# First layer's MLP in two phases of block products, by way of DRAM, and pooling evicted straight to its result

## The chip, the core and the metric

The kernel runs on one core of one Trainium2 chip. The metric is the device time of one execution in microseconds (us), median over runs. TensorE (PE in the profile) multiplies matrices into PSUM; VectorE (DVE), ScalarE (ACT) and GpSimd (POOL) do the elementwise work; SyncE (SP) only issues DMAs.

## The reference

Two layers act on 512 latent and 256 context tokens of width 1024, in fp32. The parts that the change touches:

```python
def multiscale_pool(u, w_grp, scale):            # windows 2, 4, 8, 16; one per group of 128 channels
    ug = u.reshape(B, L, POOL_GROUPS, POOL_GW)
    ...                                          # cs: running sums along the tokens
        means.append((csg[:, hi] - csg[:, lo]) / (hi - lo).astype(F32)[:, None])
    pooled = jnp.stack(means, axis=2).astype(u.dtype)
    mixed = jnp.einsum('blgc,gcd->blgd', pooled - ug, w_grp)

def sq_relu_mlp(h, w1, w2):                      # w1: 1024 x 4096, w2: 4096 x 1024
    return jnp.square(jax.nn.relu(h @ w1)) @ w2

for l in range(DEPTH):                           # DEPTH = 2
    ...                                          # mixers: retention, pooling, attention, then w_out
    x = x + g1 * mix
    x = x + g2 * sq_relu_mlp(modulate(rmsnorm(x, norm2_w[l]), sh2, sc2), w_mlp1[l], w_mlp2[l])
    if not last:                                 # the same for the context tokens
        xc = xc + cg2 * sq_relu_mlp(modulate(rmsnorm(xc, norm2_w[l]), csh2, csc2), w_mlp1[l], w_mlp2[l])
```

## The kernel before

Every fp32 product is three matmuls (`mm3`, L309): each operand is split into a rounded high part (`wh`, `uh`, made by ACT) and the rest (`wl`, `ul`, made by DVE or POOL), and high x high, high x low and low x high are added in PSUM.

`Weights` (L95) streams all weights in the order of a plan. `next` hands out the slab of the step that begins, issues the DMAs up to three steps ahead on SP's queue, and lines up the splits up to two steps ahead; `tick`, called between products, emits one piece of such a split: an ACT copy (L150) and a subtraction (L151), each 512 wide. `combine` (L163) forms sums of weight blocks on POOL, 1024 wide. Raw slabs have 6 buffers, `wh` and `wl` 3 each. Large tiles come from a pool of 11 buffers (`big`).

In layer 0 all 768 tokens go through the MLP. The hidden width 4096 is cut into 8 chunks of 512. `mlp_order` (L212) alternates: `m1` makes one chunk of the first product (per weight slab of 128 hidden channels, 8 contraction tiles, for 512 and for 256 tokens; tile `ph`, ACT evicts, squares), then `s2` (`strassen`, L1205) multiplies the chunk by its part of `w_mlp2` as 2x2 blocks in 7 block products in place of 8 (tile `st`, operands `ob`, added into `acc` by DVE). Chunks 6 and 7 go through `m2` without that. `fold` adds the result to the residual. The context and latent rows are parked in DRAM (`xk`) and read back (`xq`).

Ahead of it, output product and norm run in two groups of tiles, (0,1,2,3) and (4,5). `early` lets the MLP's first products, which need group 1 alone, run before group 2 is normalised. Beside the MLP the next layer's modulation weights (`adaw`, 24 loads of 1 MB) are loaded on POOL's queue and multiplied (`ada`).

`pool_gen` (L678) makes the pooling input: per group 48 matmuls into PSUM (`pu`), ACT evicts them to a scratch tile `up` of one buffer (L694), DVE builds window sums from it (`ps`, L703 and L706), scales and subtracts into `pm` (L711) and mends the ends (L714, L715). The next group's eviction needs `up` free.

Of the kernel before, what the change touches and what calls it, by code (L numbers as in the profile page):

```python
# [17 lines left out]
P = 128  # L18
# [14 lines left out]
NSC = 6  # L33

# [14 lines left out]
def kernel(  # L49
# [45 lines left out]
    class Weights:  # L95
# [10 lines left out]
        def add(self, key, src, pre=None, name=None):  # L106
            self.plan.append((key, src if isinstance(src, tuple) else (src,), pre, name or len(self.plan)))
# [15 lines left out]
        def dma(self, upto):  # L123
            while self.nd <= min(upto, len(self.plan) - 1):
                key, src, pre, name = self.plan[self.nd]
                if pre is None:
                    self.load(name, src)
                else:
                    for nm, ap in pre[0]:
                        self.load(nm, (ap,))  # L130
                self.nd += 1

        def split(self, upto):
            while self.ns <= min(upto, len(self.plan) - 1):
                i = self.ns
                src = self.plan[i][1][0]
                m = src.shape[1] * src.shape[2]
                box = {}
                key, _, pre, name = self.plan[i]
                if pre is not None and pre[1]:  # L140
                    self.bg.append((i, lambda pre=pre: self.combine(pre[1])))
                eng = V if key[0] == "s2" or key[0] in ("m1", "m2") and not (key[0] == "m1" and key[1:3] == (1, 0) and key[3] > 1) or key[:2] == ("t", 0) and key[2] < C_AK else nc.gpsimd

                def piece(i=i, a=0, b=512, box=box, eng=eng, name=name):
# [4 lines left out]
                    r = self.raw[name]  # L149
                    A.activation(out=box["h"][:, a:b], in_=r[:, a:b], func=AF.Copy)  # L150
                    eng.tensor_tensor(out=box["l"][:, a:b], in0=r[:, a:b], in1=box["h"][:, a:b].bitcast(F32), op=ALU.subtract)  # L151

                for a in range(0, m, 512):
                    half = key[0] == "out" or key[0] in ("m1", "m2") and key[1] == 0 or key[:3] == ("t", 0, C_RV + 256)
                    e = {"eng": nc.gpsimd if a else V} if half else {}
                    self.bg.append((i, lambda a=a, piece=piece, e=e: piece(a=a, b=a + 512, **e)))
                self.ns += 1

        def combine(self, op):
            o, a, b, f = op  # L160
            t = wp.tile([P, 1024], F32, name=f"wr{self.nr}", tag="raw", bufs=6)
            self.nr += 1
            nc.gpsimd.tensor_tensor(out=t, in0=self.raw[a], in1=self.raw[b], op=f)  # L163
            self.raw[o] = t
# [46 lines left out]

    def mlp_order(l):  # L212
        if l in STR:
            o = [("m1", 0)]
            for ch in range(1, NSC):
                o += [("m1", ch), ("s2", ch - 1)]
            o += [("s2", NSC - 1), ("fold",), ("m1", 6), ("m1", 7)]
            return o + [("m2", 6, g) for g in (NG[0] if l == 0 else mlp2_groups(l, 6))]
        o = []
        for ch in range(8):  # L220
            o.append(("m1", ch))
            if 0 < ch < 7:
                o.append(("m2", ch - 1, mlp2_groups(l, ch - 1)[0]))
        if l == 0:
            o += [("m2", 6, g) for g in NG[0]]
        else:
            o.append(("m2", 6, mlp2_groups(l, 6)[0]))
        return o

    for l in range(DEPTH):  # L230
# [17 lines left out]
        for gr in NG[l]:  # L248
            for cb in range(2):
                for kq in range(4):  # L250
                    W.add(("out", l, gr, cb, kq), wslab(w_out[l], kq * 256, 2, cb * 512, 512))
        for o in mlp_order(l):
            if o[0] == "fold":
                continue
            if o[0] == "s2":
                q = [[wslab(w_mlp2[l], o[1] * CHUNK + kh * 256, 2, c * 512, 512) for c in range(2)] for kh in range(2)]
                nm = lambda x: (l, o[1], x)
                sub, b11, b12, b21, b22, t1, t2, t3, t4 = ALU.subtract, *(nm(x) for x in ("11", "12", "21", "22", "t1", "t2", "t3", "t4"))
                for pq, loads, op, of in ((1, [(b11, q[0][0])], None, b11), (5, [(b12, q[0][1])], (t1, b12, b11, sub), t1),
                                          (6, [(b22, q[1][1])], (t2, b22, t1, sub), t2), (3, [], None, b22),  # L260
                                          (7, [], (t3, b22, b12, sub), t3), (2, [(b21, q[1][0])], None, b21),
                                          (4, [], (t4, b21, t2, sub), t4)):
                    W.add(("s2", l, o[1], pq), q[0][0], (loads, op), of)
# [76 lines left out]
    def ada(l, v, c0, n, ps_pool, ps_tag, wk, loads=None, eng1=None):  # L340
# [4 lines left out]
        if eng1 is not None:  # L345
            g = ada_dve(l, v, c0, wk, eng1)
            while acc is None:
                try:
# [3 lines left out]
                    acc = e.value  # L352
        pa = None
# [6 lines left out]
        for s, (rv, ins) in enumerate(() if acc else loads or ada_load(l, v, c0, n, nc.gpsimd)):  # L360
# [157 lines left out]
    def layer(l, u_in):  # L518
# [159 lines left out]
        def pool_gen(*gs):  # L678
            for g in gs:
                wh, wl = W.next(("pu", l, g))  # L680
                up = wk.tile([P, 800], F32, name=f"up{g}", tag="up", bufs=1)
                V.memset(up[:, 0:8], 0.0)
                V.memset(up[:, 520:536], 0.0)
                if not last:
                    V.memset(up[:, 792:800], 0.0)
                for t0, n in groups:
# [6 lines left out]
                    o = 8 if t0 == 0 else 536  # L693
# [3 lines left out]
                src, lo, hi = up, 0, (536 if last else 800)  # L697
                for s in range(g + 1):
                    st = 1 if s == 0 else 1 << (s - 1)
                    dst = wk.tile([P, 800], F32, name=f"ps{g}{s}", tag=f"pls{s % 2}")  # L700
                    if s == 0:
                        lo += 1
                        V.tensor_tensor(out=dst[:, lo:hi], in0=src[:, lo - 1 : hi - 1], in1=src[:, lo:hi], op=ALU.add)  # L703
                    else:
                        lo, hi = lo + st, hi - st
                        V.tensor_tensor(out=dst[:, lo:hi], in0=src[:, lo - st : hi - st], in1=src[:, lo + st : hi + st], op=ALU.add)  # L706
                    src = dst
                for t0, n in groups:
# [486 lines left out]
        u2h = [bigt(f"u2h{l}{q}", F32R) for q in range(2)]  # L1195
        u2l = [bigt(f"u2l{l}{q}", F32R) for q in range(2)]
# [6 lines left out]
        acc = {}  # L1203

# [149 lines left out]
        for q, gr in enumerate(NG[l]):  # L1354
# [6 lines left out]
        early()  # L1361
# [34 lines left out]
    def norm_mod(ts, xns, q, a, sh, uh, ul, wk, psp, tag):  # L1396
# [3 lines left out]
        u = wk.tile([P, 2, 256], F32, name=f"un{ts[0]}{q}", tag="un", bufs=unb[0])  # L1400
# [15 lines left out]

    def norm_group(ts, xts, a, sh, uh, ul, wk, psp, tag):
# [84 lines left out]
```

## Time and profile before

| | |
|---|---|
| median of 3 runs | 2147.99 us (2147.91 to 2148.69) |
| the profiled execution | 2149.35 us, its span 2147.6 us |
| busy share | PE 97%, weight loads 83%, DVE 61%, ACT 40%, POOL 29% |
| granted TensorE clock, mean | 0.991 |
| layer 0, MLP in full flow (791 to 1235 us) | 444 us |

The trace is of one execution; its rows give start, duration, engine, source line and tile (`out<-in`). A matmul's shown duration covers its way through the array, so neighbouring matmuls overlap in the rows: the pace of PE is the distance from start to start.

### The profile page before, as it was taken

To read this page: it belongs to the slowest core of one execution; us is meant where nothing else is said; L and a number is where in the kernel's file an instruction comes from. 1 tells how busy PE (TensorE), PEld (TensorE's weight loads), DVE (VectorE), ACT (ScalarE), POOL (GpSimd) and SP (SyncE) were. 2 spreads that over 40 slices of the span, in tenths; PEclk is the share of its full clock that TensorE was granted. 3 is DMA by queue.
4 is the path that set the end of the run, shared out by engine and by line. 5 is a ranking of instruction groups with operands and counts; after the bars stand their busy time and mean duration, and the time that the engine had idled before them with its cause. 6 is when DMAs were issued, how large, how long until landed. Compare 5 with 4: busy or idle time off the path is not lost.

```text
span 2147.6 us, 32806 instructions
## 1 busy us (share of the span) xinstructions
PE 2083.2 (97%) x12879; PEld 1775.8 (83%) x12879; DVE 1315.7 (61%) x2542; ACT 856.2 (40%) x1710; POOL 613.4 (29%) x475
## 2 busy tenths in 40 slices
PE   6999979999999999999999999998999999999999
PEld 5789968888888888888888888997888888887777
DVE  4577973455443654446569547479465267778884
ACT  4323423443432354434343335233444345654441
POOL 0342242212223331232322123433323353221300
PEclk9999989999999999999999999999999999999999
DMA  8841111111124444244426233212222164233241
GB/s 267 313 149 49 38 45 50 45 40 50 40 60 160 157 136 148 86 141 128 131 97 214 71 137 108 79 47 60 77 60 70 54 217 122 89 97 118 77 129 49
DMA packets 224692, 225.77 MB, mean 105 GB/s; under 512 B 8417, under 2 KB 180761, under 8 KB 224537
## 3 DMA queue, kind: packets, MB, share of 16 engines
q1 hardware_dynamic: 208936, 168.96, 25.2%
q0 software_dynamic: 15600, 54.71, 7.2%
q8 instruction: 101, 1.65, 0.3%
q14 instruction: 55, 0.44, 0.1%
HBM read 216.27 MB, written 7.37 MB: 104 GB/s over the span
## 4 chain that ended last, share of the span: by engine, by line
PE 80%; DVE 13%; issue 2%; DMA 2%; ACT 2%; SPq 1%; POOL 0%; DVEq 0%; ACTq 0%; POOLq 0%
PE ph L310 7%; PE ph L311 7%; PE ph L312 7%; PE pg L310 5%; PE pg L311 5%; PE pg L312 5%; PE tg L311 4%; PE tg L310 4%; PE tg L312 4%; PE st L310 4%; PE st L311 3%; PE st L312 3%; PE pb L311 3%; PE pb L310 3%; PE pb L312 3%
## 5 line engine op out<-in xcount | busy, mean ns | idle before, releaser
L151 POOL TENSOR_TENSOR wl<-wr,wh 128x512 fp32r<-128x512 f32 x304 | 414.5, 1376 | 998.9 <-ACT wh L150 930.9
L150 ACT ACTIVATE wh<-wr 128x512 fp32r<-128x512 f32 x640 | 369.9, 623 | 582.9 <-issue 243.1
L151 DVE TENSOR_TENSOR wl<-wr,wh 128x512 fp32r<-128x512 f32 x336 | 238.8, 733 | 256.4 <-ACT wh L150 256.1
L311 PE MATMUL ph<-u2l,wh 128*128 128x512 f32 (+1 forms) x808 | 279.0, 346 | 0.9 <-DVE u2l L1415 0.9
L310 PE MATMUL ph<-u2h,wh 128*128 128x512 f32 (+1 forms) x808 | 279.3, 348 | 0.3 <-ACT wh L150 0.3
L312 PE MATMUL ph<-u2h,wl 128*128 128x512 f32 (+1 forms) x808 | 277.4, 345 | 0.0
L310 PE MATMUL pg<-uh,wh 128*128 128x512 f32 (+1 forms) x576 | 206.9, 359 | 0.0
L311 PE MATMUL pg<-ul,wh 128*128 128x512 f32 (+1 forms) x576 | 206.3, 358 | 0.0
L312 PE MATMUL pg<-uh,wl 128*128 128x512 f32 (+1 forms) x576 | 205.7, 357 | 0.0
L163 POOL TENSOR_TENSOR wr<-wr,wr 128x1024 f32<-128x1024 f32 x48 | 116.8, 2434 | 259.0 <-DVE wl L151 207.3
L310 PE MATMUL st<-wh,ob 128*128 128x512 f32 x420 | 165.3, 398 | 5.8 <-DVE acc L1261 3.0
L310 PEld LDWEIGHTS ph<-u2h,wh 128*128 128x128 f32 x808 | 152.1, 189 | 22.3 <-issue 2.8
L311 PEld LDWEIGHTS ph<-u2l,wh 128*128 128x128 f32 x808 | 152.9, 189 | 19.6 <-DVE u2l L1415 1.3
L312 PEld LDWEIGHTS ph<-u2h,wl 128*128 128x128 f32 x808 | 152.9, 189 | 18.8
L311 PE MATMUL st<-wl,ob 128*128 128x512 f32 x420 | 164.7, 392 | 1.2 <-DVE wl L151 1.2
L312 PE MATMUL st<-wh,ob 128*128 128x512 f32 x420 | 164.2, 391 | 0.0
L310 PEld LDWEIGHTS pg<-uh,wh 128*128 128x128 f32 x576 | 108.9, 189 | 15.6 <-issue 1.4
L312 PEld LDWEIGHTS pg<-uh,wl 128*128 128x128 f32 x576 | 108.8, 189 | 15.4 <-issue 1.2
L310 PE MATMUL tg<-wh,uh 128*128 128x256 f32 x416 | 120.9, 291 | 0.0
L311 PEld LDWEIGHTS pg<-ul,wh 128*128 128x128 f32 x576 | 108.9, 189 | 14.4 <-issue 1.0
L311 PE MATMUL tg<-wl,uh 128*128 128x256 f32 x416 | 118.2, 284 | 0.0
L312 PE MATMUL tg<-wh,ul 128*128 128x256 f32 x416 | 117.7, 283 | 0.0
(322 smaller groups left out, 4396.9 us busy)
## 6 DMA issues: line engine op xcount, KB each, us to landing
wr<-in_w_mlp_dram SPq DMA_DIRECT2D x136, 512.0 KB, 4.1
adaw<-in_ada_w_dram POOLq DMA_DIRECT2D x42, 1024.0 KB, 7.4
wr<-in_w_in_dram SPq DMA_DIRECT2D x76, 512.0 KB, 3.8
wr<-in_w_out_dram SPq DMA_DIRECT2D x32, 512.0 KB, 3.3
wr<-in_w_in_dram SPq DMA_DIRECT2D x32, 256.0 KB, 4.2
adaw<-in_ada_w_dram SPq DMA_DIRECT2D x6, 1024.0 KB, 10.4
wr<-in_w_ret_out_dram SPq DMA_DIRECT2D x16, 256.0 KB, 2.9
wr<-in_w_pool_out_dram SPq DMA_DIRECT2D x16, 256.0 KB, 2.9
```

What stands on the lines that cost most here:

```text
L150: A.activation(out=box["h"][:, a:b], in_=r[:, a:b], func=AF.Copy)
L151: eng.tensor_tensor(out=box["l"][:, a:b], in0=r[:, a:b], in1=box["h"][:, a:b].bitcast(F32), op=ALU.subtract)
L163: nc.gpsimd.tensor_tensor(out=t, in0=self.raw[a], in1=self.raw[b], op=f)
L310: T.matmul(ps, ah, bh, start=first, stop=False, **kw)
L311: T.matmul(ps, ah, bl, start=False, stop=False, **kw)
L312: T.matmul(ps, al, bh, start=False, stop=last, **kw)
```

## The change

In layer 0 alone (`SA = (0,)`):

- Phase `s1`, 8 chunks in a row: the first product too as 7 block products, halves of the 768 tokens (384 a matmul) by halves of the contraction. Seven token operands `ub`, each split into high and low, are made once, the first two after norm group 1, the other five after group 2; norm groups are now (0,1,2) and (3,4,5). Weight blocks are summed on POOL, 512 wide. The hidden result `ht` goes to DRAM (`hd`, 8 stores of 1.5 MB, SP).
- Phase `s3`: three pairs of chunks, read back (`hr`, SP), 1024 hidden rows a pass: the same 252 matmuls a pair as two `s2`, but one addition into `acc` where there were two. Half of the `wl` pieces go to POOL. Then `fold`, and `m2` of chunks 6 and 7, whose `hr` is split by `split67`.
- The 24 loads of `adaw` move to SP's queue.

In both layers the pooling input is evicted straight into `pm`; the first window sum reads it in two parts with single columns copied; `up` is gone.

Counted over the program: 720 matmuls of 512 columns and 864 of 256 columns leave the first product, 1344 of 384 come; DVE has 33 instructions more (63 additions into `acc` fewer), ACT 6 fewer, POOL 90 more (50 `wl`, 64 sums of 512; 24 DMAs fewer), SP 40 more.

```diff
+SA = (0,)
...
     def mlp_order(l):
+        if l in SA:
+            o = [("s1", ch) for ch in range(8)] + [("s3", ch) for ch in range(0, NSC, 2)] + [("fold",)]
+            return o + [("m2", 6, g) for g in (NG[0] if l == 0 else mlp2_groups(l, 6))]
...
+                eng = V if key[0] in ("s1", "s2", "s3") or key[0] in ("m1", "m2") and not (...
+                half = key[0] == "out" or ... or key[0] == "s1" and key[3] > 1 or key[0] == "s3"
...
+                    e = (nc.gpsimd if a else V) if half else eng
...
+                for q in range(2):
+                    ops = [(ra[q], r1[q], r1[q], add, 0, 0, 512, 512), (ra[q], ra[q], r0[q], sub, 512, 0, 0, 512)]
+                    W.add(("s1", l, o[1], 2 + q), slab[0], ([(r1[q], slab[2 * q + 1])], ops), parts=...
...
-        for s, (rv, ins) in enumerate(() if acc else loads or ada_load(l, v, c0, n, nc.gpsimd)):
+        for s, (rv, ins) in enumerate(() if acc else loads or ada_load(l, v, c0, n, nc.sync if l and 0 in SA else nc.gpsimd)):
...
-                    A.activation(out=up[:, o : o + n], in_=pu[:, :n], func=AF.Copy)
+                    A.activation(out=pm[:, g, t0 : t0 + n], in_=pu[:, :n], func=AF.Copy)
...
+        def operands(part):
...
+                for k in (slice(0, 2), slice(2, 4)):
+                    if sm:
+                        V.tensor_tensor(out=blk[:, k], in0=sm[0][:, k], in1=sm[1][:, k], op=ALU.subtract)
+                    A.activation(out=o[:, 0, k], in_=blk[:, k], func=AF.Copy)
+                    V.tensor_tensor(out=o[:, 1, k], in0=blk[:, k], in1=o[:, 0, k].bitcast(F32), op=ALU.subtract)
...
+        def s1(ch):
+            ht = big.tile([P, 4, ntok], F32, name=f"ht{l}{ch}", tag="big")
+            seq = [[(1, 0), (2, 0)], [(1, 1), (2, 1)], [(5, 0), (6, 0)], [(5, 1), (6, 1)], [(7, 0), (3, 0)], [(7, 1), (3, 1)], [(4, 0), (4, 1)]]
+            for e, prods in enumerate(seq):
+                wh, wl = W.next(("s1", l, ch, e))
+                for hf, (pq, q) in enumerate(prods):
...
+                    for k in range(4):
+                        mm3(bk, wh[:, 4 * hf + k, :], wl[:, 4 * hf + k, :], ub[pq][:, 0, k], ub[pq][:, 1, k], ...
...
+                    if pq in (1, 5, 6, 4):
+                        A.activation(out=hv, in_=bk, func=AF.Copy)
+                    else:
+                        V.tensor_tensor(out=hv, in0=bk, in1=hv, op=ALU.add)
+                    if pq in (3, 4):
+                        hf2 = ht[:, 2 * q + f, :]
+                        V.scalar_tensor_tensor(out=hf2, in0=hf2, scalar=0.0, in1=hf2, op0=ALU.max, op1=ALU.mult)
...
+            nc.sync.dma_start(out=hd[ch], in_=ht.rearrange("p a b -> p (a b)"))
...
+        def strassen2(ch):
+            for c in range(ch, min(ch + 4, NSC)):
+                load_h(c)
...
+                for h in range(2):
+                    wh, wl = W.next(("s3", l, ch, pq, h))
...
+                        if h:
...
+                            if (t, cb) in seen:
+                                V.tensor_tensor(out=av, in0=bk, in1=av, op=ALU.add)
```

The order of the instructions, at three places of layer 0. First ACT at the pooling input (`up` scratch, `pm` result, `pu` PSUM of PE, `pq` and `QS` the queries of the attention, `pg` and `y` a gate). Before:

```order
L694 ACTIVATE up_2924<-pu_2968 128x256
L150 ACTIVATE wh_3125<-wr_3010 128x512
L694 ACTIVATE up_3012<-pu_3016 128x512
L694 ACTIVATE up_3012<-pu_3060 128x256
L150 ACTIVATE wh_3192<-wr_3106 128x512 x2
L694 ACTIVATE up_3108<-pu_3112 128x512
L694 ACTIVATE up_3108<-pu_3142 128x256
L1068 ACTIVATE QS_3264<-pq_3261 64x256
```

After:

```order
L725 ACTIVATE pm_1367<-pu_2968 128x256
L725 ACTIVATE pm_1367<-pu_3020 128x512
L155 ACTIVATE wh_3133<-wr_3018 128x512
L725 ACTIVATE pm_1367<-pu_3064 128x256
L725 ACTIVATE pm_1367<-pu_3120 128x512
L155 ACTIVATE wh_3208<-wr_3118 128x512 x2
L725 ACTIVATE pm_1367<-pu_3150 128x256
L976 ACTIVATE y_3192<-pg_3195 128x512
```

The evictions no longer write one scratch tile in turn, and the gate `y` now stands ahead of the queries `QS`.

Second DVE at the start of the MLP, the second norm group (`xn` the scaled rows, `xt` their transposes in PSUM, `u2l` and `ub` the split operands). Before:

```order
L1394 TENSOR_SCALAR xn_7625<-xr_6925,rs_7628 128x1024
L1394 TENSOR_SCALAR xn_7626<-xr_6925,rs_7628 128x1024
L1415 TENSOR_TENSOR u2l_6939<-un_7317,u2h_6937 128x2x256
L1415 TENSOR_TENSOR u2l_6939<-un_7327,u2h_6937 128x2x256
L1409 TENSOR_SCALAR un_7649<-xt_7648,cols_69 128x256
L1409 TENSOR_SCALAR un_7659<-xt_7658,cols_69 128x256
L1415 TENSOR_TENSOR u2l_6938<-un_7649,u2h_6936 128x2x256
```

After:

```order
L1258 TENSOR_TENSOR uf_6952<-uf_6952 128x2x384 x2
L1585 TENSOR_SCALAR uf_6953<-xt_7647,cols_69 128x256
L1585 TENSOR_SCALAR uf_6953<-xt_7654,cols_69 128x256
L1260 TENSOR_TENSOR ub_7661<-uf_6952,ub_7661 128x768 x2
L1258 TENSOR_TENSOR uf_6952<-uf_6953,uf_6952 128x2x384
L443 COPY wcol_72<-lct_7709 128x68
L1258 TENSOR_TENSOR uf_6952<-uf_6953,uf_6952 128x2x384 x3
L1258 TENSOR_TENSOR uf_6953<-uf_6953,uf_6952 128x2x384
L1260 TENSOR_TENSOR ub_7668<-uf_6952,ub_7668 128x768
L1260 TENSOR_TENSOR ub_7675<-uf_6952,ub_7675 128x768
L1258 TENSOR_TENSOR uf_6953<-uf_6953,uf_6952 128x2x384
```

Where two splits of 512 columns followed each pair of scaled blocks, 18 operations of 768 columns (8 differences `uf`, 10 splits `ub`) now follow the whole norm on DVE.

Third POOL in the second product (`wr` raw weights, L163 and L167 their sums). Before, one chunk of `s2`:

```order
L163 TENSOR_TENSOR wr_8142<-wr_8065,wr_8001 128x1024
L151 TENSOR_TENSOR wl_7934<-wr_7836,wh_7933 128x512
L163 TENSOR_TENSOR wr_8231<-wr_8127,wr_8142 128x1024
L338 DMA adaw_8061<-in_ada_w_dram 128x4x512
L338 DMA adaw_8161<-in_ada_w_dram 128x4x512
L151 TENSOR_TENSOR wl_8017<-wr_7918,wh_8016 128x512
L163 TENSOR_TENSOR wr_8321<-wr_8127,wr_8065 128x1024
L163 TENSOR_TENSOR wr_8385<-wr_8312,wr_8231 128x1024
```

After, in a pair of `s3`:

```order
L167 TENSOR_TENSOR wr_10377<-wr_10452,wr_10377 128x1024
L167 TENSOR_TENSOR wr_10452<-wr_10558,wr_10452 128x1024
L156 TENSOR_TENSOR wl_10462<-wr_10426,wh_10461 128x512
L167 TENSOR_TENSOR wr_10426<-wr_10528,wr_10426 128x1024
L156 TENSOR_TENSOR wl_10546<-wr_10377,wh_10545 128x512
L167 TENSOR_TENSOR wr_10528<-wr_10595,wr_10528 128x1024
L167 TENSOR_TENSOR wr_10377<-wr_10558,wr_10377 128x1024
L156 TENSOR_TENSOR wl_10576<-wr_10426,wh_10575 128x512
L167 TENSOR_TENSOR wr_10426<-wr_10595,wr_10426 128x1024
```

A chunk has four sums as before; the issues of `adaw` are gone, and POOL now has one `wl` for each of the 14 weight slabs of a pair.

## Rows read from the trace of the kernel before

**Rows 1.** The page's first part: busy us, share of the span, instructions.

```profile
PE 2083.2 (97%) x12879; PEld 1775.8 (83%) x12879; DVE 1315.7 (61%) x2542; ACT 856.2 (40%) x1710; POOL 613.4 (29%) x475
```

**Rows 2.** Busy us by stretch: PE, PEld, DVE, ACT, POOL; granted clock; DMA share, GB/s.

```profile
288.00:294.00 6.00, 6.00 (x27) 5.83 (x28) 5.61 (x19) 0.86 (x3) 0.08 (x1) 0.51 0.01 3
...
740.00:756.00 16.00, 14.85 (x74) 12.05 (x73) 15.05 (x26) 7.28 (x14) 6.65 (x6) 1.00 0.69 192
756.00:791.00 35.00, 32.72 (x239) 30.48 (x238) 19.91 (x45) 22.62 (x48) 10.17 (x12) 1.00 0.53 182
791.00:1235.00 444.00, 444.00 (x2950) 373.92 (x2949) 262.05 (x358) 172.61 (x309) 120.09 (x91) 1.00 0.38 123
```

**Rows 3.** Timeline, PE, start and duration: `tg` of 512 columns.

```profile
749.32 0.39 PE L310 MATMUL tg<-wh,yh 128*128 128x512 f32 x1
...
750.90 0.39 PE L311 MATMUL tg<-wl,yh 128*128 128x512 f32 x1
```

**Rows 4.** Timeline, PE: `ph` of 256 columns.

```profile
832.10 0.28 PE L311 MATMUL ph<-u2l,wh 128*128 128x256 f32 x1
...
833.66 0.28 PE L312 MATMUL ph<-u2h,wl 128*128 128x256 f32 x1
```

**Rows 5.** Waits between 255 and 310 us: total us, times, longest.

```profile
PE pu L310 <- ACT up L694: 9.5, 1, 9.5
...
DVE ps L703 <- ACT up L694: 6.0, 2, 5.1
```

**Rows 6.** Timeline, PE, 276 to 317 us, idle in brackets.

```profile
287.85 0.58 PE L310 MATMUL pu<-uh,wh 128*128 128x256 f32 x1 [9.54 <-ACT up L694]
...
315.67 0.40 PE L1094 MATMUL S<-KS,QS 128*128 128x256 f32 x2
```

**Rows 7.** Timeline, DVE, the end of the pooling.

```profile
303.94 0.99 DVE L703 TENSOR_TENSOR ps<-up 128x799 f32<-128x799 f32 x1 [5.06 <-ACT up L694]
...
307.08 0.28 DVE L715 TENSOR_TENSOR pm<-pm,up 128x1 f32<-128x1 f32 x2
```

**Rows 8.** Timeline, DVE, second norm group.

```profile
760.02 0.68 DVE L1190 TENSOR_TENSOR xr<-xr,rt 128x512 f32<-128x512 f32 x1
...
766.82 1.42 DVE L1394 TENSOR_SCALAR xn<-xr,rs 128x1024 f32<-128x1024 f32 x2
...
770.79 0.99 DVE L1409 TENSOR_SCALAR un<-xt,cols 128x256 f32<-128x256 f32 x2 [1.36 <-PE xt L1403]
```

**Rows 9.** Groups of DVE, 791 to 1235 us: busy us, mean ns, idle before.

```profile
L1261 DVE TENSOR_TENSOR acc<-st,acc 128x512 f32<-128x512 f32 x114 | 76.8, 683 | 15.6 <-PE st L312 14.9
...
L1232 DVE TENSOR_TENSOR ob<-hb,ob 128x768 fp32r<-128x768 f32 x24 | 25.8, 1077 | 18.8 <-ACT ob L1231 18.8
L1232 DVE TENSOR_TENSOR ob<-stt,ob 128x768 fp32r<-128x768 f32 x18 | 23.4, 1300 | 16.2 <-ACT ob L1231 16.1
```

**Rows 10.** Groups of POOL, same stretch.

```profile
L163 POOL TENSOR_TENSOR wr<-wr,wr 128x1024 f32<-128x1024 f32 x24 | 58.1, 2420 | 88.8 <-DVE wl L151 53.4 <-issue 34.6
L151 POOL TENSOR_TENSOR wl<-wr,wh 128x512 fp32r<-128x512 f32 x29 | 38.4, 1323 | 122.6 <-ACT wh L150 122.6
```

**Rows 11.** Timeline, DVE, in a second product.

```profile
844.42 0.96 DVE L1232 TENSOR_TENSOR ob<-hb,ob 128x768 fp32r<-128x768 f32 x1 [2.82 <-ACT ob L1231]
...
856.83 0.69 DVE L151 TENSOR_TENSOR wl<-wr,wh 128x512 fp32r<-128x512 f32 x1
```

**Rows 12.** Timeline, POOL, 278 to 284 us.

```profile
277.01 3.38 POOL L151 TENSOR_TENSOR wl<-wr,wh 128x512 fp32r<-128x512 f32 x2
```

**Rows 13.** Timeline, DVE, the same stretch.

```profile
279.19 1.74 DVE L855 TENSOR_TENSOR tbn<-aq,ropeB 128x512 f32<-128x512 f32 x1
```

**Rows 14.** DMA issues: KB each, us to landing (DMA view).

```profile
adaw<-in_ada_w_dram SPq DMA_DIRECT2D x6, 1024.0 KB, 10.4
...
xq<-xk SPq DMA_DIRECT2D x6, 512.0 KB, 7.9
```

**Rows 15.** The page's fifth part: weight loads.

```profile
L310 PEld LDWEIGHTS ph<-u2h,wh 128*128 128x128 f32 x808 | 152.1, 189 | 22.3 <-issue 2.8
```

More of the change, by code (lines that the diff above doesn't have):

```diff
@@ L138, in split, with piece @@
                 box = {}
[L139 to L144, printed above, removed]
+                key, _, pre, parts, _ = self.plan[i]
+                for op in pre[1] if pre is not None else ():
+                    self.bg.append((i, lambda op=op: self.combine(*op)))
+                for nm, ap in pre[2] if pre is not None and len(pre) > 2 else ():
+                    self.bg.append((i, lambda nm=nm, ap=ap: self.load(nm, (ap,))))
+                eng = V if key[0] in ("s1", "s2", "s3") or key[0] in ("m1", "m2") and not (key[0] == "m1" and key[1:3] == (1, 0) and key[3] > 1) or key[:2] == ("t", 0) and key[2] < C_AK else nc.gpsimd
+                half = key[0] == "out" or key[0] in ("m1", "m2") and key[1] == 0 or key[:3] == ("t", 0, C_RV + 256) or key[0] == "s1" and key[3] > 1 or key[0] == "s3"
+                def piece(a, rn, off, eng, i=i, box=box):
                     if not box:
@@ L148, in piece, with combine @@
                         self.sp[i] = (box["h"], box["l"])
[L149 to L156, printed above, removed]
-                self.ns += 1
[L159 to L164, printed above, removed]
+                    r = self.raw[rn][:, off : off + 512]
+                    A.activation(out=box["h"][:, a : a + 512], in_=r, func=AF.Copy)
+                    eng.tensor_tensor(out=box["l"][:, a : a + 512], in0=r, in1=box["h"][:, a : a + 512].bitcast(F32), op=ALU.subtract)
+                for a, (rn, off) in zip(range(0, m, 512), parts):
+                    e = (nc.gpsimd if a else V) if half else eng
+                    self.bg.append((i, lambda a=a, rn=rn, off=off, e=e, piece=piece: piece(a, rn, off, e)))
+                self.ns += 1
+        def combine(self, o, a, b, f, oo=0, ao=0, bo=0, n=1024):
+            if o not in self.raw:
+                self.raw[o] = wp.tile([P, 1024], F32, name=f"wr{self.nr}", tag="raw", bufs=6)
+                self.nr += 1
+            nc.gpsimd.tensor_tensor(out=self.raw[o][:, oo : oo + n], in0=self.raw[a][:, ao : ao + n], in1=self.raw[b][:, bo : bo + n], op=f)
         def start(self):
@@ L1194, in layer @@
         ylk = lambda k: yl[k // 4][:, k % 4, :]
-        u2h = [bigt(f"u2h{l}{q}", F32R) for q in range(2)]
-        u2l = [bigt(f"u2l{l}{q}", F32R) for q in range(2)]
+        sa = l in SA
+        if sa:
+            u2h, u2l = [bigt(f"uf{l}{q}") for q in range(2)], None
+        else:
+            u2h = [bigt(f"u2h{l}{q}", F32R) for q in range(2)]
+            u2l = [bigt(f"u2l{l}{q}", F32R) for q in range(2)]
         u2hk = lambda k: u2h[k // 4][:, k % 4, :]
@@ new lines, in load_h, with split67 @@
+        def load_h(ch):
+            if sa and ch not in hs:
+                hs[ch] = big.tile([P, 4, ntok], F32, name=f"hr{l}{ch}", tag="big")
+                nc.sync.dma_start(out=hs[ch].rearrange("p a b -> p (a b)"), in_=hd[ch])
+        def split67():
+            for ch in (6, 7):
+                load_h(ch)
+            for ch in (6, 7):
+                r = hs[ch]
+                hh, hl_ = bigt(f"hh{l}{ch}", F32R), bigt(f"hl{l}{ch}", F32R)
+                hs[ch] = (hh, hl_)
+                for j in range(4):
+                    A.activation(out=hh[:, j, :ntok], in_=r[:, j, :], func=AF.Copy)
+                    V.tensor_tensor(out=hl_[:, j, :ntok], in0=r[:, j, :], in1=hh[:, j, :ntok].bitcast(F32), op=ALU.subtract)
@@ new lines, in strassen2, with prep @@
+        def strassen2(ch):
+            for c in range(ch, min(ch + 4, NSC)):
+                load_h(c)
+            hb = hs.pop(ch), hs.pop(ch + 1)
+            tmp = [wk.tile([P, 2, HT], F32, name=f"stt{l}{ch}{h}", tag="un", bufs=unb[0]) for h in range(2)]
+            add, sub = ALU.add, ALU.subtract
+            order = (1, 5, 6, 3, 7, 2, 4)
+            ob = {}
+            def prep(q):
+                pq = order[q]
+                o = ob[pq] = big.tile([P, 2, 4, HT], F32R, name=f"ob{l}{ch}{pq}", tag="big")
+                for h in range(2):
+                    k = slice(2 * h, 2 * h + 2)
+                    blk = lambda th, kh: hb[kh][:, k, th * HT : th * HT + HT]
+                    pre = {5: (tmp[h], blk(1, 0), blk(1, 1), add), 6: (tmp[h], tmp[h], blk(0, 0), sub), 3: (tmp[h], blk(0, 1), tmp[h], sub),
+                           7: (blk(1, 0), blk(0, 0), blk(1, 0), sub)}
+                    src = {1: blk(0, 0), 2: blk(0, 1), 4: blk(1, 1)}.get(pq)
+                    if src is None:
+                        src, a, b, f = pre[pq]
+                        V.tensor_tensor(out=src, in0=a, in1=b, op=f)
+                    A.activation(out=o[:, 0, k], in_=src, func=AF.Copy)
+                    V.tensor_tensor(out=o[:, 1, k], in0=src, in1=o[:, 0, k].bitcast(F32), op=sub)
+            dst = {1: (0, 0), 5: (1, 1), 6: (0, 1), 3: (0, 1), 7: (1, 1), 2: (0, 0), 4: (1, 0)}
+            chain = {1: "x", 6: "x", 7: "x", 4: "x", 5: "y", 3: "y", 2: "z"}
+            banks = {}
+            if not acc:
+                ab = [big.tile([P, 3, DM], F32, name=f"acc{l}{q}", tag="big") for q in range(1 if last else 2)]
+                acc[0] = [xr[1][:, 1 + t, :] if last and t < 2 else ab[(t - 2) // 3 if last else t // 3][:, (t - 2) % 3 if last else t % 3, :] for t in tiles]
+            seen = acc.setdefault("seen", set())
+            prep(0)
+            prep(1)
+            for q, pq in enumerate(order):
+                if q + 2 < 7:
+                    prep(q + 2)
+                elif q == 5 and ch + 2 == NSC:
+                    split67()
+                for h in range(2):
+                    wh, wl = W.next(("s3", l, ch, pq, h))
+                    for i in range(nu):
+                        key = chain[pq], i
+                        new = key not in banks
+                        if new:
+                            banks[key] = ps.tile([P, 512], F32, name=f"st{l}{ch}{pq}{i}", tag="g")
+                        bk = banks[key]
+                        c = slice(i * P, i * P + P)
+                        for k in range(2):
+                            kk = 2 * h + k
+                            mm3(bk, ob[pq][:, 0, kk, c], ob[pq][:, 1, kk, c], wh[:, k, :], wl[:, k, :], new and kk == 0, kk == 3, skip_group_check=True)
+                        if h:
+                            th, cb = dst[pq]
+                            t = th * nu + i
+                            av = acc[0][t][:, cb * 512 : cb * 512 + 512]
+                            if (t, cb) in seen:
+                                V.tensor_tensor(out=av, in0=bk, in1=av, op=ALU.add)
+                            else:
+                                seen.add((t, cb))
+                                A.activation(out=av, in_=bk, func=AF.Copy)
+                        W.tick()
+                        yield 6 * 512 / 2400.0
@@ L1329, in mlp_gen @@
                     yield from strassen(o[1])
+                elif o[0] == "s1":
+                    yield from s1(o[1])
+                elif o[0] == "s3":
+                    yield from strassen2(o[1])
                 elif o[0] == "fold":
@@ L1360, in layer @@
             norm_group(gr, [xr[t // 3][:, t % 3, :] for t in gr], cl[:, 3], cl[:, 2], u2h, u2l, wk, ps, "t")
-        early()
+            if sa:
+                operands(q)
+        if not sa:
+            early()
         if strass and not last:
```

123 lines of the change are left out of this document (89 added, 34 removed).

## The prediction

> **What bounds the kernel now.** I read the shares of the engines first: PE is busy 97% of the span [rows 1]; so time is gained by giving PE less to do, or by closing its few gaps. Then the stretches of layer 0: in the MLP in full flow PE never rests, DVE works 59% of the time, POOL 27%, and the DMA engines 38% at 123 GB/s [rows 2]. Then PE's pace, start to start: seven steps of 512 columns take 1.58 us, 0.226 each [rows 3]; thirteen of 256 take 1.56, 0.120 each [rows 4]. Then the waits around the one long gap: PE waits 9.5 us for ACT's eviction into `up`, and DVE in its turn twice for the next `up` [rows 5]. Last DVE and POOL, because the change gives POOL more to do and both share work on the weights [rows 9 to 13].
>
> 0.2% (4.3 us) is about what a measurement can tell from no change. The sum is made against the profiled execution, 2149.35 us, 1.36 above the median of the runs.
>
> **The first product.** 720 matmuls of 512 columns and 864 of 256 leave: 720 x 0.2265 + 864 x 0.120 = 267 us. 1344 of 384 come. No row has that width; between the two paces [rows 3, 4] a straight line gives 0.1735 us, so 233 us: **-33.9**. Bounds: 0.170 (three quarters of the 512 pace) gives -38.5, 0.180 (one and a half of the 256 pace) -25. The line is nearest, since both rows lie on it. PE is the bound here, so all of it shows as long as the operands come in time. The second product keeps its 252 matmuls a pair: 0.
>
> On the weight loads: one takes 189 ns in the rows [rows 15], longer than my 0.1735, yet 256-column matmuls with such loads ran 0.120 apart [rows 4], so loads overlap one another. The Trainium skill (Perfetto Trace Analysis, "Identifying the Most-Contended Engine") would judge TensorE by the busy share of its weight loads rather than of its matmuls; 1344 x 0.189 = 254 us would then bound the phase and the sum would gain 13 in place of 34. Rows 4 speak against it here.
>
> **The pooling input.** PE's gap of 9.54 us ends at 287.85 [rows 6]; after it the clock is at 0.51 for 6 us [rows 2], which costs 2.9 more. Without both PE would stand at its second S product at 315.67 - 12.4 = 303.2 [rows 6]. DVE is next in the way: the queries `QS` stand behind the pooling on DVE. Its last pooling step ends at 307.36 [rows 7]; without the 6.0 us for `up` [rows 5] 301.4. Added are 16 one-column copies and 4 more additions, 20 instructions; at the 0.14 of a one-column step [rows 7] 2.8 us, and `QS` itself takes some 0.6. So S can start near 304.8, and PE, with all its other work ahead of that done, gains 10.9 less what a wait of 2 us does to the clock: **-9** (-13 if the DVE ops shorten too, -4 if DVE's waits on POOL, below, grow by what it saved). In layer 1 PE doesn't wait for `up`: -1.
>
> **The start of the MLP.** Before, the second norm group hides well: PE idles 1.15 and 2.28 us in the two stretches around it [rows 2]. From the last residual (760.70) to the scaled rows (768.24) are 7.5 us, to the first transposed block on DVE 10 [rows 8]. In the change 48 matmuls (8.3 us) and 24 transposes (3) are all that PE has. The first new operand needs a third scaled tile (0.7), the blocks, two differences and two splits at 0.96 [rows 11]: some 17 us from the last residual, 20 from the last output matmul, so PE idles 9. Fourteen operations follow on DVE at 0.96 to 1.3 [rows 9, 11], 14 to 18 us for four more operands, of which PE uses one in 24 x 0.1735 = 4.2 us: 5 more. 14 less the 3.4 of before, and a little clock: **+11** (+5 if the orders interleave well, +17 if each operation takes 1.3).
>
> **Phase s1 otherwise.** A weight slab now has 24 matmuls, 4.2 us. A chunk (29 us) asks of POOL 8 sums of 512 (half of 2.42) and 5 `wl` of 1.32 [rows 10], 16.3 us, of DVE 9 `wl`, 6 additions and 4 squares, some 14. Both fit, with a lead of two slabs. Three sums in a slab's chain can bite at places: **+3** (0 to +8).
>
> **From s1 to s3, and the fold.** Eight stores and eight reads of 1.5 MB come. Around the last chunk four reads, the weights and `adaw` make about 9.5 MB on SP's queue; at the 182 to 192 GB/s that the busiest of these stretches moved [rows 2] some 50 us, longer than the 29 of that chunk, though the reads of the second pair aren't needed for another 57. A read of 512 KB landed after 7.9 us, `adaw` on SP after 10.4 [rows 14]; the 24 loads moved to SP stand among the weight loads there. **+2** (0 to +20).
>
> **Phase s3: POOL against DVE.** Here is the new load. Two rows show how they share: POOL ran `wl` until 280.39 [rows 12], DVE's operation issued at 279.19 ended at 280.93, 1.74 in place of 0.68, and 0.54 after POOL [rows 13]. The splits `ob`, 0.96 alone [rows 11], average 1.08 and 1.30 [rows 9]. So a DVE operation on two SBUF tiles waits out POOL's. Additions from PSUM stay at 0.683 [rows 9]. A pair of chunks, 57.2 us of PE, holds 8 sums of 2.42 and 14 `wl` of 1.32 on POOL [rows 10], 37.9 us, and on DVE 14 `wl` of 0.54 and 22 operations of 0.82 (0.68 and 0.96 less the 0.14 that the wait hides), 25.6: together 63.5. `ada` products stretch PE's side by a few us, and the lead helps once: **+6** over three pairs (0 if they interleave, +34 with whole durations: 68.5 a pair).
>
> Sum: -33.9 - 9 - 1 + 11 + 3 + 2 + 6 = -21.9: 2127.4 for a profiled execution, **2126** as a median.
>
> **Rivals.**
>
> *The covers hold* (0.18): start +5, s1, transition and s3 nothing, pooling -11: 2149.35 - 33.9 - 11 - 1 + 5 = 2108, 2107 as a median. For it: in full flow PE never waited though DVE and POOL collided [rows 2, 9].
>
> *DVE behind POOL in all of s3, slower than before* (0.10): DVE has 14 x 0.68 + 22 x 0.96 + 21 additions x 0.683 = 45 us of its own a pair. If each of the 36 two-tile operations waits 1.06 as in rows 13, that is 83 us against 57.2: +77 for three pairs in place of +6, 2197. It is slower than before from 9.5 us lost a pair (0.26 of wait an operation beyond balance), and then every weight slab and operand is late. Against it: the mean excess in rows 9 is 0.12 to 0.34, with POOL half as busy. The Trainium skill (SBUF — State Buffer, "SBUF: two separate sides") says that the two share a port pair as an exclusive lock; rows 12 and 13 agree.
>
> *The way through DRAM is late* (0.06): +20 in place of +2, 2144; for it the burst on one queue, against it DMA at 38% of its time.
>
> *Weight loads bound the first product* (0.02): 2126 + 21 = 2147, unchanged. Against it rows 4. The rule above gives this.
>
> *The change doesn't shorten `pu`'s wait* (0.04): DVE, not `up`, is what PE waits for; +9, 2135, still faster.
>
> **How the numbers follow.** Forecast 0.60 (its own range 2112 to 2142). Faster: 0.60 + 0.18 + 0.04 and half of the DRAM case, less a tail of the forecast, 0.82. Same: the weight loads, the other half, that tail: 0.07. Slower: 0.10 and a little: 0.11. The range takes in the covers and the DRAM case: 2104 to 2149.
>
> **What would show it.** `sp` matmuls 0.1735 apart; no wait of PE for ACT at `pu`, S near 305; a gap of about 14 us in pieces after the last output product; in s3 PE busy with short waits for `wl` or `ob`, DVE operations near 1.5 us. The forecast is wrong if `sp` runs slower than 0.180, if s1 shows a wait in each slab, or if the second product takes over 65 us a pair.

## The result and the profile after

The changed kernel takes 2163.76 us (2162.69 to 2163.84) against 2148.34 us (2147.91 to 2149.90) of the kernel before on the same chip: a ratio of 1.0071, interval 1.0058 to 1.0083. It is slower by 15 us; 22 us faster had been forecast, and the time lies above the stated range. The profiled execution has a span of 2160.7 us, 13.1 more than before.

The page's first part answers to [rows 1]: PE is busy 10 us less, POOL 185 us more, DVE 116 us more although it has only 33 more instructions.

```profile
PE 2073.5 (96%) x12639; PEld 1780.8 (82%) x12639; DVE 1431.4 (66%) x2575; ACT 863.0 (40%) x1704; POOL 798.3 (37%) x565
```

The places where the 13.1 us arose, from the starts of the first and last matmuls of a stage:

| us | before | after |
|---|---|---|
| start of the MLP in layer 0 (first `ph` or `sp`) | 756.3 | 746.6 |
| MLP, to the first `tw` of layer 1 | 547.2 | 566.4 |
| of it first product, to the first `st` | | 271.9 |
| of it second product, first to last `st` | | 222.9 |
| of it chunks 6 and 7, last `st` to first `tw` | | 71.5 |
| from the first `tw` to the end | 844.1 | 847.7 |

Up to the MLP 9.7 us are gained, in it 19.2 lost, behind it 3.6 lost. The stretches of the changed kernel, columns as in [rows 2]: the start of the MLP, the rest of the first product, the second product.

```profile
746.60:771.00 24.40, 15.42 (x75) 13.06 (x73) 20.32 (x39) 12.02 (x24) 8.77 (x10) 0.73 0.54 174
771.00:1018.00 247.00, 245.51 (x1749) 235.17 (x1749) 167.43 (x172) 94.74 (x177) 158.06 (x103) 0.99 0.56 186
1018.00:1242.00 224.00, 201.35 (x1115) 158.57 (x1114) 196.79 (x184) 92.11 (x149) 138.05 (x74) 0.95 0.45 165
```

The first product keeps PE busy (245.5 of 247). The second product doesn't: 201 of 224 us, at a clock of 0.95, with POOL at 62% of the time, where the full flow before had 27% and no gap [rows 2]. POOL's share alone doesn't tell the two apart: in the first product it is 64%.

The new matmuls of 384 columns keep the pace that the straight line gave: from 746.61 to 748.54 eleven steps, 1.93 us, 0.175 each; over the whole phase the median is 0.173.

```profile
746.61 0.33 PE L346 MATMUL sp<-ub,wh 128*128 128x384 f32 x1
...
748.54 0.33 PE L348 MATMUL sp<-ub,wl 128*128 128x384 f32 x1
...
754.78 0.34 PE L348 MATMUL sp<-ub,wl 128*128 128x384 f32 x1
```

At the pooling, PE no longer waits for ACT at `pu`; it waits for DVE's queries, 4.3 us, and the first S product starts at 304.4. PE had come there at 300.0.

```profile
PE S L1133 <- DVE QS L1108: 4.3, 1, 4.3
```

After the fourth block product (754.78, above) PE waits 7 us for the scaled rows of the second norm group:

```profile
762.10 1.12 PE L1579 MATMUL xt<-ident,xn 128*128 128x128 f32 x4 [6.98 <-DVE xn L1568]
```

In the second product DVE's operations on two SBUF tiles are stretched, the additions from PSUM (`acc<-st`) are not. Columns as in [rows 9]:

```profile
L156 DVE TENSOR_TENSOR wl<-wr,wh 128x512 fp32r<-128x512 f32 x42 | 44.4, 1065 | 11.8 <-ACT wh L155 11.7
L1332 DVE TENSOR_TENSOR ob<-stt,ob 128x768 fp32r<-128x768 f32 x18 | 36.1, 2034 | 1.2 <-ACT ob L1331 1.2
L1332 DVE TENSOR_TENSOR ob<-hr,ob 128x768 fp32r<-128x768 f32 x22 | 33.4, 1549 | 3.1 <-ACT ob L1331 3.1
L1365 DVE TENSOR_TENSOR acc<-st,acc 128x512 f32<-128x512 f32 x48 | 31.4, 681 | 8.3 <-PE st L348 8.3
L1330 DVE TENSOR_TENSOR stt<-hr,hr 128x768 f32<-128x768 f32 x6 | 13.2, 2226 | 0.0
```

`ob` alone takes 0.96 us [rows 11] and averages 2.03 and 1.55 here. POOL's groups, against 2420 and 1323 ns in [rows 10]:

```profile
L156 POOL TENSOR_TENSOR wl<-wr,wh 128x512 fp32r<-128x512 f32 x43 | 69.6, 1620 | 61.6 <-ACT wh L155 36.5 <-PE st L348 9.4 <-issue 8.0
L167 POOL TENSOR_TENSOR wr<-wr,wr 128x1024 f32<-128x1024 f32 x23 | 65.2, 2841 | 21.8 <-issue 9.7 <-DVE wl L156 7.0 <-PE ada L412 3.3
```

One such place, as timelines of POOL, DVE and PE. POOL makes three sums on end:

```profile
1033.16 9.05 POOL L167 TENSOR_TENSOR wr<-wr,wr 128x1024 f32<-128x1024 f32 x3 [3.36 <-issue]
```

In the meantime two splits of 0.96 us take 6.2 on DVE, two differences 5.0, and only then comes the `wl` for which PE has stood still since 1039. Here the two engines take turns, one operation each, so that each operation lasts nearly as long as its own work and the other's together:

```profile
1033.82 6.20 DVE L1332 TENSOR_TENSOR ob<-stt,ob 128x768 fp32r<-128x768 f32 x2
1039.94 5.03 DVE L1330 TENSOR_TENSOR stt<-hr,stt 128x768 f32<-128x768 f32 x2
1044.90 0.68 DVE L156 TENSOR_TENSOR wl<-wr,wh 128x512 fp32r<-128x512 f32 x1
```

```profile
1043.06 0.84 ACT L1331 ACTIVATE ob<-stt 128x768 fp32r<-128x768 f32 x1 [8.69 <-DVE stt L1330]
1044.29 1.14 ACT L155 ACTIVATE wh<-wr 128x512 fp32r<-128x512 f32 x2
1045.63 0.80 PE L347 MATMUL st<-wl,ob 128*128 128x512 f32 x1 [6.30 <-DVE wl L156]
```

The way to that `wl` leads over ACT as well: the copy `wh` that it needs stands on ACT behind an `ob` that waits 8.7 us for DVE's difference `stt`. Behind the gap PE runs at the lower of its two clock levels:

```profile
1045.60:1049.00 3.40, 3.37 (x18) 2.30 (x22) 3.40 (x3) 0.56 (x1) 3.40 (x2) 0.50 0.00 0
```

Elsewhere in the second product `wh` waits for POOL's sum itself, seven times, 24.4 us in all:

```profile
ACT wh L155 <- POOL wr L167: 24.4, 7, 6.2
```

### The profile page after: what moved, and what is told of

Read it like the earlier page. It is cut to its first block, busy times and chain, and to the rows that moved or that the text cites. A ratio compares the mean times of both kernels' runs of the same rounds, so it can differ in the third digit from the quotient of the medians.

```text
span 2160.7 us, 32609 instructions
## 1 busy us (share of the span) xinstructions
PE 2073.5 (96%) x12639; PEld 1780.8 (82%) x12639; DVE 1431.4 (66%) x2575; ACT 863.0 (40%) x1704; POOL 798.3 (37%) x565
## 5 line engine op out<-in xcount | busy, mean ns | idle before, releaser
L156 POOL TENSOR_TENSOR wl<-wr,wh 128x512 fp32r<-128x512 f32 x354 | 502.2, 1430 | 987.3 <-ACT wh L155 884.6
L155 ACT ACTIVATE wh<-wr 128x512 fp32r<-128x512 f32 x688 | 398.0, 623 | 631.6 <-issue 251.8
L156 DVE TENSOR_TENSOR wl<-wr,wh 128x512 fp32r<-128x512 f32 x334 | 284.8, 871 | 181.5 <-ACT wh L155 181.2
L167 POOL TENSOR_TENSOR wr<-wr,wr 128x512 f32<-128x512 f32 (+1 forms) x96 | 211.7, 2219 | 198.7 <-DVE wl L156 167.3
L347 PE MATMUL st<-wl,ob 128*128 128x512 f32 x420 | 169.4, 404 | 20.7 <-DVE wl L156 20.5
L346 PE MATMUL sp<-ub,wh 128*128 128x384 f32 x448 | 151.4, 343 | 1.3 <-DVE ht L1285 0.6
L347 PE MATMUL sp<-ub,wh 128*128 128x384 f32 x448 | 151.2, 338 | 0.5 <-DVE ub L1260 0.4
L348 PE MATMUL sp<-ub,wl 128*128 128x384 f32 x448 | 150.3, 337 | 0.0
L347 PEld LDWEIGHTS st<-wl,ob 128*128 128x128 f32 x420 | 81.3, 194 | 41.8 <-DVE wl L156 24.2
L346 PEld LDWEIGHTS st<-wh,ob 128*128 128x128 f32 x420 | 81.0, 193 | 29.4 <-DVE acc L1428 4.6
L347 PE MATMUL ph<-u2l,wh 128*128 128x512 f32 (+1 forms) x280 | 103.7, 372 | 0.3 <-DVE u2l L1591 0.3
```

The lines of the kernel that those rows point to most:

```text
L155: A.activation(out=box["h"][:, a : a + 512], in_=r, func=AF.Copy)
L156: eng.tensor_tensor(out=box["l"][:, a : a + 512], in0=r, in1=box["h"][:, a : a + 512].bitcast(F32), op=ALU.subtract)
L167: nc.gpsimd.tensor_tensor(out=self.raw[o][:, oo : oo + n], in0=self.raw[a][:, ao : ao + n], in1=self.raw[b][:, bo : bo + n], op=f)
L346: T.matmul(ps, ah, bh, start=first, stop=False, **kw)
L347: T.matmul(ps, ah, bl, start=False, stop=False, **kw)
L348: T.matmul(ps, al, bh, start=False, stop=last, **kw)
```

## The experiments

Theory: DVE's operations on two SBUF tiles and POOL's exclude each other, and since each engine works in order, the `wl` that PE needs stands behind operand work that waits for POOL. Rivals: the reads from DRAM come late; DVE has too much work of its own. A third, that POOL's sums are late by POOL's own slowness, whatever DVE does, has no run that separates it: every run below that takes work from POOL relieves both. For each run the stages are measured as in the table above.

| run | median us | ratio to before (interval) | MLP us | second product us | first `tw` to end us |
|---|---|---|---|---|---|
| `pool_only` | 2144.48 | 0.9982 (0.9973 to 0.9992) | 547.2 | | 847.1 |
| `s3_no_sums` | 2138.38 | 0.9955 (0.9940 to 0.9970) | 540.5 | 195.5 | 847.7 |
| `s3_wl_dve` | 2147.71 | 0.9995 (0.9986 to 1.0005) | 549.6 | 204.9 | 845.6 |
| `hr_twice` | 2172.01 | 1.0108 (1.0093 to 1.0123) | 577.4 | 221.2 | 847.7 |
| `pool_l0` | 2141.53 | 0.9968 (0.9957 to 0.9979) | 547.1 | | 844.1 |
| `s3_quiet` | 2128.77 | 0.9908 (0.9895 to 0.9922) | 529.9 | 186.7 | 847.5 |
| `s3_sums_dve` | 2144.23 | 0.9981 (0.9972 to 0.9990) | 547.6 | 200.3 | 846.0 |
| `s3_wl_dve_l0` | 2145.20 | 0.9982 (0.9973 to 0.9991) | 550.1 | 204.7 | 843.7 |
| `s3_mix_l0` | 2140.87 | 0.9965 (0.9952 to 0.9979) | 546.9 | 201.9 | 844.0 |
| `s3_all_dve_l0` | 2137.01 | 0.9947 (0.9934 to 0.9959) | 543.0 | 198.4 | 843.7 |
| `pool_l0_again` | 2141.41 | 0.9968 (0.9955 to 0.9980) | 547.1 | | 844.0 |

**One part alone, `pool_only`.**

```diff
-SA = (0,)
+SA = ()
```

> The pooling part alone, the MLP as before. The pooling gap: PE reached the second S product 9.2 us earlier in the changed kernel. If that part stands by itself: 2139 us, between 2136 and 2142, and S in layer 0 at 304 to 305 us. If the order of the MLP's operations had helped there: 2148 us.

2144.5, 2.5 us above the first case and 3.5 below the second; S starts at 304.1, as the first case said. In the trace the MLP starts at 748.3, 8.1 us earlier than before, but from the first `tw` to the end the kernel takes 847.1 us, 3.0 more than before: layer 1 loses with this part. One row of it is a wait that ends at 1481.8 us, 6.2 us long; before it was 5.2:

```profile
PE pb L346 <- ACT y L976: 6.2, 1, 6.2
```

**The part in layer 0 only, `pool_l0`.** The pooling code is chosen by layer:

```diff
+        pool_gen = pool_gen_up if l else pool_gen_direct
```

> The pooling part in layer 0 alone, layer 1's pooling and the whole MLP as before. With the part in both layers, layer 0 gained 8.1 us in the trace and the end of layer 1 lost 3.0. Theory (layer 1's part costs those 3): 2140 to 2142 us. Rival (the 3 us come from how PE's later work falls, whatever the pooling there does): 2143 to 2145 as with both.

2141.5, and 844.1 us behind the first `tw`, exactly as before: the first case. So layer 1's share of this edit costs time: over all the traces the stretch takes 845.6 to 847.7 us with it and 843.7 to 844.1 without. How its longer wait for ACT's `y` comes about, and where the rest of the loss lies, was not followed further.

**POOL without the sums, `s3_no_sums`.**

```diff
-                        op = [tuple(x[h] for x in ops[pq]) + (ALU.subtract,)] if pq in ops else []
+                        op = []
```

> The 24 sums of 1024 that POOL makes in the second product are left out (the weight blocks are multiplied as loaded, so the result is not the reference's); loads, reads from DRAM and DVE's own operations stay. Theory (DVE's two-tile operations wait for POOL, and PE for DVE's wl): of the 38 us that the second product lost most comes back, 2163.8 falls to 2125 to 2138, and DVE's ob splits fall from 1.5 and 2.0 us to under 1.3. Rival (the reads from DRAM come late): the time stays within 5 us of 2163.8. Rival (DVE's own work is too much): under 10 us come back.

2138.4, 0.4 us above the theory's range: the second product falls from 222.9 to 195.5 us, while the reads from DRAM are all there, and the splits `ob` average 1.09 us, under the 1.3 that was expected. The rivals of late reads and of DVE's own work fail. One stall of 7 us stays, and it is the exclusion the other way round. From 1032.9 to 1043.8 DVE runs operation on operation, 13 that begin after POOL's `wl` has, and this one `wl`, 1.27 us alone, takes 12.0. The two behind it take 1.27 each (the second view gives the shortest, the median and the longest in ns):

```profile
1032.91 14.44 POOL L156 TENSOR_TENSOR wl<-wr,wh 128x512 fp32r<-128x512 f32 x3 [5.21 <-ACT wh L155]
```

```profile
L156 POOL TENSOR_TENSOR wl<-wr,wh x3: 1268/1274/11973, 1032.9 to 1046.1; 128x512 fp32r<-128x512 f32 x3
```

**All `wl` back on DVE, `s3_wl_dve`.**

```diff
-                half = ... or key[0] == "s1" and key[3] > 1 or key[0] == "s3"
+                half = ... or key[0] == "s1" and key[3] > 1
```

> The 42 wl pieces of the second product that the change gave POOL go back to DVE. Theory (time under the shared access counts): POOL's 1.3 to 1.6 us each leave and 0.68 on DVE come, together 63.5 us a pair falls to some 55, so 10 to 25 us come back: 2140 to 2154. Rival (DVE's own work is the bound): DVE's own 45 us a pair grows to 54, nothing comes back or it gets slower: 2160 to 2175. Rival (DRAM): 2163.8 within 3.

2147.7, in the theory's range, and outside both rivals': DVE gets 42 operations more, and its busy time falls, from 196.8 us of 224 (above) to 186.6 of 204:

```profile
1025.00:1229.00 204.00, 192.81 (x1105) 153.65 (x1104) 186.55 (x224) 91.05 (x147) 79.38 (x33) 0.97 0.50 181
```

**The reads twice, `hr_twice`.**

```diff
+                for _ in range(2):
-                nc.sync.dma_start(out=hs[ch].rearrange("p a b -> p (a b)"), in_=hd[ch])
+                    nc.sync.dma_start(out=hs[ch].rearrange("p a b -> p (a b)"), in_=hd[ch])
```

> Each of the eight reads of 1.5 MB from DRAM is made twice. Rival (the way through DRAM is late, landing after 16 us): the second product loses 15 us more or beyond, 2178 and over. Theory (DVE against POOL): a wait of a few us at the first pair, 2164 to 2171.

2172.0, between the two. The trace decides: the second product is no longer (221.2), nearly all of the loss lies ahead of it, where the first product's stage grows from 271.9 to 283.1 because ACT, and PE behind it, wait for the first pair:

```profile
PE st L346 <- ACT ob L1332: 9.1, 1, 9.1
ACT ob L1332 <- DMA hr<-hd: 6.7, 1, 6.7
```

So the reads have little to spare at that place. As the change makes them ACT waits 3.6 us for the first pair and PE not at all, so they aren't what delays it.

**POOL silent, `s3_quiet`.** The edits of `s3_no_sums` and `s3_wl_dve` together.

> Second product without the POOL sums (blocks multiplied as loaded, the result is not the reference's) and with all wl on DVE: POOL does nothing there. Theory (the loss is the two engines waiting for one another): only DVE's own 54 us a pair against 57 of PE is left, so the second product falls from 223 to 184 to 192 us, 2122 to 2133 in all. Rival (DVE's own work is what is too much): 200 us or more, 2140 and over.

2128.8, as the theory said: the second product takes 186.7 us, and PE works all of it at full clock:

```profile
1019.00:1206.00 187.00, 187.00 (x1110) 152.17 (x1109) 154.39 (x221) 90.09 (x145) 6.79 (x10) 1.00 0.56 199
```

This is the size of the loss: 222.9 - 186.7 = 36 us from POOL's work in the second product. What remains for DVE here, without the sums, fits beside PE.

**The sums on DVE, `s3_sums_dve`.**

```diff
-... + (ALU.subtract,)] if pq in ops else []
+... + (ALU.subtract, 0, 0, 0, 1024, V)] if pq in ops else []
```

(`combine` takes the engine as its last argument.)

> The sums of the second product on DVE, half of wl left on POOL, result as the reference's. DVE's own work is 45 + 8 x 1.2 = 55 us a pair, POOL's 18.5. Theory (waits for one another, POOL's long sums worst): a DVE operation now meets at most 1.3 us of POOL: 2140 to 2152. Rival (DVE's sheer work): 2160 to 2175, since it gets 10 us a pair more.

2144.2, as the theory had it: DVE gets some 10 us a pair more to do, and the second product is 22.6 us shorter.

**Both corrections, `s3_wl_dve_l0`.**

> The change with wl of the second product on DVE and the pooling part in layer 0 alone. If the two corrections add: 2147.7 less 3 is 2145, between 2142 and 2147. If layer 1 loses 2 to 3 us for another reason: 2147 to 2149.

2145.2, in the first case: they add, with 204.7 us in the second product as before the second correction and 843.7 behind the first `tw`.

**Between and beyond, `s3_mix_l0`, `s3_all_dve_l0`, `pool_l0_again`.** Sums on DVE in both; of `wl` a quarter on POOL (`key[0] == "s3" and key[4] == 0`) or none.

> Sums of the second product on DVE, a quarter of its wl (every second slab's second half) on POOL, pooling part in layer 0 alone. With half of wl on POOL the second product took 200 us, with POOL silent and no sums 187. Theory (each two-tile meeting of the engines costs): 192 to 199 us for the second product, 2134 to 2141 in all. Rival (DVE's sheer work is now the bound, since it gets 5 us a pair more): 200 us or more, 2142 and over.

> Sums and all wl of the second product on DVE, POOL silent there, pooling part in layer 0 alone. DVE's own work is then about 64 us a pair against 57 of PE and some 4 of ada products. If DVE's sheer work sets the pace: 195 to 205 us for the second product, 2137 to 2147. If waits for POOL were all there was: 187 to 192, 2129 to 2134.

> The pooling part in layer 0 alone, on the same chip as the two kernels beside it, to compare them: 2140 to 2142 us by the run before.

The pooling part alone gives 2141.4 again. The mix gives 2140.9 and 201.9 us in the second product: the total lies in the theory's range, the stage in the rival's. Without POOL 2137.0 and 198.4: taking 21 `wl` from POOL and giving them to DVE, the fuller engine, saves 3.5 us. The mix's trace has one large stall, of the kind of `s3_no_sums`: DVE runs without a pause from 1034.9 to 1052.7, and one `wl` of POOL in this time takes 14.4 us:

```profile
L156 POOL TENSOR_TENSOR wl<-wr,wh x2: 1269/7819/14369, 1039.5 to 1053.8; 128x512 fp32r<-128x512 f32 x2
```

```profile
1053.90 0.80 PE L347 MATMUL st<-wl,ob 128*128 128x512 f32 x1 [9.57 <-POOL wl L156]
```

Without POOL DVE works 178 of 197 us, its operations have their lone durations, and PE is nearly without gaps:

```profile
1018.00:1215.00 197.00, 193.95 (x1106) 153.25 (x1105) 177.66 (x246) 90.87 (x147) 5.39 (x9) 0.98 0.53 190
```

```profile
L156 DVE TENSOR_TENSOR wl<-wr,wh 128x512 fp32r<-128x512 f32 x83 | 53.8, 683 | 13.8 <-ACT wh L155 13.7
...
L167 DVE TENSOR_TENSOR wr<-wr,wr 128x1024 f32<-128x1024 f32 x24 | 29.0, 1214 | 0.0
L1373 DVE TENSOR_TENSOR ob<-hr,ob 128x768 fp32r<-128x768 f32 x22 | 20.3, 949 | 0.6 <-ACT ob L1372 0.6
```

Time and stage lie where DVE's sheer work was expected to put them. That it is the cause isn't shown: PE's idle time is one wait for DVE's copy `adar` (1.7 us) and one for a load of `adaw` (1.3), none for `wl` or `ob`. Against `s3_quiet`, from start to start, the `st` matmuls take 6.4 us more, `ada` 3.8 and `adat` 1.6; why was not followed. This version, the change with the second product's weights all on DVE and the pooling in layer 0, is the fastest of those that leave nothing out: 0.9947 of before, and 4.4 us under the pooling part alone on the same chip.

## Why the prediction was wrong

**The first product** held: 0.1735 a matmul was forecast, 0.173 is the median. The rival of weight loads, which would have bounded the phase at 254 us, fails with rows of this kernel: the 1344 matmuls ran at 0.173, under the 0.189 of one load.

**The pooling input** held in layer 0: S at 304.4 against 304.8; the MLP starts 8.1 us earlier (`pool_only`), 9.2 (`pool_l0`) or 7.3 (`pool_l0_again`) against -9, and the medians fall by 7.6 and 6.7 with the part in layer 0 alone. The near match of S has some luck in it: PE was ready at 300.0 and not at 303.2, so it waited 4.3 us for DVE where some 2 had been reckoned. In layer 1 -1 was forecast, because PE doesn't wait for `up` there; it cost +1.5 to +3.6. That no wait is removed doesn't mean that none is added.

**The start, phase s1, the way through DRAM** held as a sum: without POOL's work in the second product the MLP takes 529.9 us, 17.2 less than before; -33.9 + 11 + 3 + 2 = -17.9 had been summed. The single terms were not measured apart. At the start PE idles 9.0 us, 7.0 of them after the fourth block product, where 9 were forecast for that place; of the 5 more for the later operands hardly any came. The clock was 0.73 in the first 24.4 us; what that cost was not measured apart. Phase s1, with PE busy 245.5 of 247 us, took less than +3.

**Phase s3** is the step that failed: "+6 over three pairs", where 36 us came (222.9 against the 186.7 of `s3_quiet`). The mechanism was named, with the rows that show it [rows 12, 13], and +34 stood there as the upper end; the size was wrong. I added up the time in which either engine needs the access, 63.5 us a pair, and set it against PE's 57.2 as if the turns cost nothing beyond that time. They do: whichever waits also delays all that stands behind it, its work that needs no shared access too, and behind DVE's operand work stand ACT's copies and the `wl` of the next slab. DVE's waiting can be estimated: `s3_quiet` has 154.4 us of DVE at lone durations, less the 42 `wl` of 0.68 that POOL makes in the change 126, and the change has 196.8, so about 71 us of the second product went into waits. The loss has two parts: gaps of PE (224 - 201 = 23 us) and, behind the gaps, PE at half clock (0.95 on average, where `s3_quiet` has 1.00; about 11 us). The prediction's own sign was right: over 65 us a pair for the second product meant a wrong forecast, and it took 74.

**The rivals.** The one on the other side, DVE behind POOL in s3 and slower than before, is what happened, with a chance of 0.10 and a price of +77 where 36 came. The evidence against it, a mean excess of 0.12 to 0.34 us in [rows 9], came from a stretch in which POOL was busy 27% of the time; at 62% the excess of `ob` is 0.6 and 1.1. The prediction noted that POOL had been half as busy, but let the old excess stand against the rival; even twice it, 0.24 to 0.68, reaches the 0.60 a wait (0.34 to DVE's balance with PE and 0.26 beyond) from which the rival is slower than before. Late DRAM and bound weight loads did not occur, nor did the covers all hold; at `pu` PE's wait for ACT went, and a shorter one for DVE came.

The sum with the two mended terms (layer 1 as +3, s3 as +36) and the others as forecast: -33.9 - 9 + 3 + 11 + 3 + 2 + 36 = +12.1; the span grew by 13.1.

## What to carry to other kernels

Where two engines exclude each other, work moved from the busier to the idler one need not be relief: here DVE with 24 to 66 more operations finished the stretch sooner than with POOL's help. The time for which both need the access doesn't price such a move: by an estimate from lone durations (0.68 and 0.95 us an operation on DVE, 1.29 on POOL) it came to about 80% of the first product here, where PE lost next to nothing, and of the second product in `s3_no_sums`, where one stall of 7 us stayed. Ask instead what stands behind an operation that waits, on an engine that works in order, and how soon it is needed. Here the pace of a new matmul width followed from its neighbours; whether the saving arrived depended on the engines that make the operands.

## What the runs showed of the hardware

DVE's operations on two SBUF tiles and POOL's delay each other in both directions. At the place shown from the changed kernel they take turns: two operations of DVE of 0.96 us took 6.2 during POOL's sums. While DVE worked without a break, one POOL operation of 1.27 us took 12.0 (`s3_no_sums`) and one took 14.4 (`s3_mix_l0`). What decides between turns and such a long wait no run here shows. DVE additions with one operand in PSUM were untouched (681 ns, beside POOL at 62%). The Trainium skill (SBUF — State Buffer, "SBUF: two separate sides") describes the pair of ports as an exclusive lock: whichever of the two operations starts first has it for the whole instruction, and the other blocks fully. The turns agree. The long waits go beyond it: in `s3_no_sums` POOL's `wl`, which began at 1032.91, ended only after 13 operations of DVE that began later.

Matmuls with 384 columns fall on the line between 256 and 512: 0.120, 0.173, 0.227 us, about 13 ns over the columns at 2.4 GHz in each case.
